# Seven smaller products for a second factor of a Strassen-Winograd projection, with weights split through PSUM

## The chip, the cores and the metric

The kernel runs on one core of a Trainium2 chip. The metric is the device time of one execution in microseconds (us). A core has a matmul engine (TensorE, PE in the profile, with its weight loads as PEld), three engines for elementwise work (VectorE = DVE, ScalarE = ACT, GpSimd = POOL) and SyncE (SP), which issues the DMAs here. Every engine works through its own queue in order; semaphores hold an instruction until what it needs is done. Matmul results go to PSUM, which has eight banks of 128 x 512 float32; everything else lies in SBUF.

## The reference

One layer of a gated short-convolution mixer with a norm before and after. D = 1024, L = 1024 positions, the inner width CI is 2048; all in float32.

```python
def short_conv_mixer(u, w_in, conv_w, w_out):
    z, bg, cg, v = jnp.split(u @ w_in.astype(u.dtype), 4, axis=-1)
    y = bg * causal_dwconv(cg * v, conv_w) * jax.nn.silu(z)
    return y @ w_out.astype(u.dtype)

def reference(x, pre_norm, post_norm, sc_w_in, sc_conv_w, sc_w_out, ...):
    u = rms_norm(x, pre_norm[0])
    m = short_conv_mixer(u, sc_w_in[0], sc_conv_w[0], sc_w_out[0])
    return x + rms_norm(m, post_norm[0])
```

The convolution is depthwise and causal with three taps. Nearly all of the arithmetic is the two projections, 1024 x 1024 by 1024 x 8192 and 1024 x 2048 by 2048 x 1024.

## The kernel before

**Precision.** A float32 product is made of three matmuls in a rounded format (float32r): each operand is split into a high part and a low part, and lo x hi, hi x lo and hi x hi are added in one PSUM bank. `split` does it: ScalarE copies the source into the rounded high part, VectorE subtracts that from the source and leaves the low part (L157 to L159; for the weights of a pair L164 to L175, where the subtraction is L170).

**Tiling of the input projection.** CI is cut into NC = 16 chunks of 128 channels. A chunk needs four column blocks of w_in: for cg and v (the even pair p = 2c) and for z and bg (the odd pair p = 2c + 1). A pair is one 2 x 2 block product, done in Strassen-Winograd form with seven products a, b, c, e, d, f, g instead of eight (`product`, L189). Each has four K blocks times three matmuls, so twelve matmuls of 128 x 128 weights by 512 columns. The activations' combinations UH, UL (names u_a to u_g) are made once; the weights' combinations are made for each pair: `add_s` forms the sums e, c, f and the difference d on POOL (se, sc, sf and raw in the profile; L150, L152, L154, L146). `after` (L215) copies the banks out on ScalarE (`snap`) and adds later products on VectorE: L227 for d, L234 for f, L224 for b. Product f adds into bank pv, which e has begun; the result goes to sn[p, "c"].

**The second level.** From chunk DEEP = 3 on, product b of a chunk's two pairs is taken together: the two pairs' weights for b form a 2 x 2 block matrix, and seven products a' to g' of half size replace the two products. Each is six matmuls of 256 columns (`deep_product`, L728). Their weights' sums are made on POOL (`deep_sums`, ds in the profile, L706 to L710), split in `deep_prep` (dw0, dw1, dw2 of 512 columns and dw3 of 256), and the results are added on VectorE in `deep_after` (L754), which then starts the convolution of the chunk. The factor's own sums are made once under chunk 2 and chunk 3 (`deep_parts`, `deep_subs`, `deep_split`, started from the table UNDER).

**The gate.** When a chunk's even pair is ready, `start_conv` multiplies into gpad (L250 and, for the second half of the positions, L239 on POOL), ScalarE does the first tap (L634) and VectorE the two others (L640). The odd pair gives SiLU(z) (L236, L933) and bg, multiplied in on POOL (L231, L237) and VectorE (L243, L244). The result goes to DRAM (`y_done`). `add_y` then forms its sums for the output projection, one subtraction for chunks below 8 and three from 8 on, of the chunk before.

**w_out.** While the input projection runs, w_out's sums for the second Strassen-Winograd product are also formed: `fetch_t` loads blocks, `add_t` subtracts on VectorE and stores to DRAM (four subtractions per unit; units 0 to 7 are 512 columns wide, L321, units 8 to 15 are 256 wide, L308 to L316). The table TODO says at which pair each unit's turn is.

**Order.** The order of all instructions is written out by hand. The list `slots` is TensorE's order of products. The main loop goes through it: it issues a product, then `prepare(n)` issues the splits of all slots that start within LEAD = 7 (in units in which a full product is 2.72 and a small one 0.72) behind the end of this one, and then the work that follows the product. So each engine's queue follows the slots.

**Memory.** A ring of 36 pages of 128 x 512 float32 (`page`) holds weights, sums and results; a new page waits until the last reader of the one in its place is done. PSUM's eight banks go round in the same way (`bank`).

**Output projection.** Behind chunk 15 comes a second Strassen-Winograd product with y and w_out (L1023 to L1025, with two of its products again by seven smaller ones, L1115 to L1117), and the norm after it.

Of the kernel before, what the change touches and what calls it, by code (L numbers as in the profile page):

```python
# [16 lines left out]
DEEP = 3  # L17
LEAD = 7.0


@with_exitstack
def kernel(
# [144 lines left out]

    def split_low(p, i):
        hi, lo = wt[p, i]
        nc.vector.tensor_sub(lo, source(p, i), hi.bitcast(F32))  # L170

    def split_w(p, kinds):
        for i in kinds if p < len(PAIRS) else "":
            split_high(p, i)
            split_low(p, i)  # L175
# [490 lines left out]

    HH, KQ = HB // 2, KH // 2
    deep, deep_w = {}, {}

    def deep_parts(ks):  # L670

        for k in ks:
            deep[k] = page(f"deep{k}")
            nc.gpsimd.tensor_add(deep[k], UH["b"][:, k].bitcast(F32), UL["b"][:, k].bitcast(F32))

    def deep_subs(ks):

        for k in ks:
            (b11, b12), (b21, b22) = ((t[:, :HH], t[:, HH:]) for t in (deep[k], deep[k + KQ]))
# [7 lines left out]
    def deep_split(i):  # L687
# [3 lines left out]
        if i != "e'":  # L691
            deep[i] = [tmp.tile([P, KQ, HH], F32R, tag="ub", name=f"u{i[0]}{h}_deep", bufs=6) for h in "hl"]
        for k in range(KQ):
            if i == "e'":
                hi, lo = UH["b"][:, k, ls], UL["b"][:, k, ls]
            else:
                hi, lo = (t[:, k] for t in deep[i])
            split(deep[k0 + k][:, ls], hi, lo)

    def deep_sums(c, part):  # L700

        (a11, a12), (a21, a22) = ((t[:, :HH], t[:, HH:]) for t in (block(p, 0, 1) for p in (2 * c, 2 * c + 1)))
        t = page(f"ds{part}_{c}")
        deep[c, part] = t
        if part == 0:
            nc.gpsimd.tensor_add(t[:, :HH], a21, a22)  # L706
            nc.gpsimd.tensor_sub(t[:, HH:], t[:, :HH], a11)
        else:
            nc.gpsimd.tensor_sub(t[:, :HH], a11, a21)
            nc.gpsimd.tensor_sub(t[:, HH:], a12, deep[c, 0][:, HH:])  # L710
# [4 lines left out]
    def deep_prep(c, i):  # L715
        n = DEEP_W[i][0]
        if (c, n) in deep_w:
            return
        if n == 3:
            w = page(f"dw{n}_{c}", F32R, (2, HH))  # L720
            hi, lo, src = w[:, 0], w[:, 1], block(2 * c + 1, 0, 1)[:, HH:]
        else:
            hi, lo = (page(f"dw{n}{h}_{c}", F32R) for h in "hl")
            src = deep.pop((c, n - 1)) if n else block(2 * c, 0, 1)
        split(src, hi, lo)
        deep_w[c, n] = hi, lo

# [506 lines left out]
```

## Time and profile before

| | |
|---|---|
| time, median of 3 runs | 783.65 us (783.64 to 783.88) |
| the profiled execution | 783.5 us, of which span 781.7 us |
| granted TensorE clock, mean | 0.997 |
| ScalarE, POOL busy in the span | 343.2 us, 385.8 us |
| HBM read, written | 91.78 MB, 34.60 MB |

The span goes from the first to the last instruction of the program that the profiler recorded; 1.8 us lie around it. A row of the order in time has the start in us from the span's begin, the duration in us, the engine, the line, the operation, output <- inputs by the program's names (buffer numbers left out), and the shapes; in brackets the idle time before it and what ended that. A duration includes the time for which an instruction that has been started is held up inside the engine. A row of one source line has durations in ns as min/median/max.

### The profile page before, as it was taken

Reading aid. Unit: us, or ns where it says so; the run is one execution under the profiler, and the core shown is the slowest. Engines: PE = TensorE matmul, PEld = TensorE weight load, DVE = VectorE, ACT = ScalarE, POOL = GpSimd, SP = SyncE. Lnnn points to the kernel's source line nnn. Section 1 sums busy time; section 2 is a strip of 40 time slices with the busy share of each in tenths; the row PEclk is TensorE's granted clock in tenths of the full one; section 3 lists DMA queues with packets and bytes.
Section 4 is the critical chain, followed back from the end, with each engine's and each line's share of the span. In section 5 each row is a group of like instructions: output and inputs, shape, how many; then the busy total and the mean of one; then the engine's idle time right before and its main releaser. Section 6 shows DMA issues by size and latency. Waiting matters only on the chain.

```text
span 781.7 us, 11253 instructions
## 1 busy us (share of the span) xinstructions
PE 772.6 (99%) x3852; PEld 656.5 (84%) x3852; DVE 647.1 (83%) x868; ACT 343.2 (44%) x624; POOL 385.8 (49%) x281
## 2 busy tenths in 40 slices
PE   8999999999999999999999999999999999999996
PEld 7888888888888888888888888888888889889985
DVE  6899757969696989898888888896868899986975
ACT  7664434443334343434342434333333575754821
POOL 2506579647474747565565747383838200710041
PEclk9999999999999999999999999999999999999998
DMA  9210431317070738373746455552324979686355
GB/s 323 55 55 14 135 94 55 113 36 231 26 233 23 256 109 256 117 259 126 219 119 205 142 182 166 173 167 95 112 91 138 354 264 386 222 282 206 116 163 188
DMA packets 115817, 127.12 MB, mean 163 GB/s; under 512 B 7416, under 2 KB 74032, under 8 KB 115760
## 3 DMA queue, kind: packets, MB, share of 16 engines
q1 hardware_dynamic: 115744, 126.41, 50.2%
q8 instruction: 30, 0.49, 0.3%
q14 instruction: 27, 0.22, 0.1%
q10 hardware_dynamic: 16, 0.00, 0.0%
HBM read 91.78 MB, written 34.60 MB: 162 GB/s over the span
## 4 chain that ended last, share of the span: by engine, by line
PE 98%; DMA 1%; DVE 0%; ACT 0%; POOL 0%; SPq 0%; issue 0%; DVEq 0%; POOLq 0%; ACTq 0%
PE px L200 14%; PE px L201 14%; PE px L202 14%; PE pv L200 7%; PE pv L202 7%; PE pv L201 7%; PE po_x L1023 4%; PE po_x L1025 4%; PE po_x L1024 4%; PE px L745 2%; PE px L743 2%; PE px L744 2%; PE pp L422 1%; PE po_v L1025 1%; PE po_v L1023 1%; PE po_v L1024 1%
## 5 line engine op out<-in xcount | busy, mean ns | idle before, releaser
L231 POOL TENSOR_TENSOR sne<-sne,cv 128x512 f32<-128x512 f32 x15 | 25.1, 1674 | 149.9 <-DVE sne L227 134.7
L239 POOL TENSOR_TENSOR gpad<-snc,sne 128x512 f32<-128x512 f32 x15 | 25.2, 1678 | 65.8 <-DVE snc L234 65.8
L640 DVE SCALAR_TENSOR_TENSOR cv<-gpad,cw,cv 128x1024 f32<-128x1024 f32 x32 | 42.4, 1325 | 14.7 <-ACT cv L634 14.1
L170 DVE TENSOR_TENSOR wal<-raw,wah 128x512 fp32r<-128x512 f32 x31 | 29.6, 954 | 27.8 <-ACT wah L166 27.8
L152 POOL TENSOR_TENSOR sc<-se,raw 128x512 f32<-128x512 f32 x31 | 50.3, 1621 | 2.4
L154 POOL TENSOR_TENSOR sf<-raw,sc 128x512 f32<-128x512 f32 x31 | 51.4, 1657 | 0.0
L150 POOL TENSOR_TENSOR se<-raw,raw 128x512 f32<-128x512 f32 x31 | 47.3, 1525 | 3.2 <-DMA raw<-in_sc_w_in 3.2
L200 PE MATMUL px<-u_d,wdl 128*128 128x512 f32 x124 | 48.6, 392 | 0.0
L201 PE MATMUL px<-u_d,wdh 128*128 128x512 f32 x124 | 48.4, 391 | 0.0
L200 PE MATMUL px<-u_a,wal 128*128 128x512 f32 x124 | 48.4, 391 | 0.0
L200 PE MATMUL px<-u_g,wgl 128*128 128x512 f32 x124 | 48.4, 390 | 0.0
L201 PE MATMUL px<-u_g,wgh 128*128 128x512 f32 x124 | 48.4, 390 | 0.0
L201 PE MATMUL px<-u_a,wah 128*128 128x512 f32 x124 | 48.4, 390 | 0.0
L202 PE MATMUL px<-u_d,wdh 128*128 128x512 f32 x124 | 48.4, 390 | 0.0
L208 ACT COPY sna<-px 128x512 f32<-128x512 f32 x30 | 17.5, 585 | 70.2 <-PE px L202 47.5
L200 PE MATMUL pv<-u_f,wfl 128*128 128x512 f32 x124 | 48.3, 390 | 0.0
L202 PE MATMUL pv<-u_f,wfh 128*128 128x512 f32 x124 | 48.3, 389 | 0.0
L202 PE MATMUL px<-u_a,wah 128*128 128x512 f32 x124 | 48.2, 389 | 0.0
L201 PE MATMUL pv<-u_f,wfh 128*128 128x512 f32 x124 | 48.2, 389 | 0.0
L200 PE MATMUL px<-u_c,wcl 128*128 128x512 f32 x124 | 48.2, 389 | 0.0
L201 PE MATMUL px<-u_c,wch 128*128 128x512 f32 x124 | 48.2, 389 | 0.0
L202 PE MATMUL px<-u_c,wch 128*128 128x512 f32 x124 | 48.2, 389 | 0.0
(446 smaller groups left out, 2592.7 us busy)
## 6 DMA issues: line engine op xcount, KB each, us to landing
raw<-in_sc_w_in SPq DMA_DIRECT2D x128, 256.0 KB, 4.6
y_d<-cv SPq DMA_DIRECT2D x16, 512.0 KB, 3.1
s_d<-s SPq DMA_DIRECT2D x32, 256.0 KB, 3.1
t<-in_sc_w_out SPq DMA_DIRECT2D x32, 256.0 KB, 4.4
t_d<-t SPq DMA_DIRECT2D x32, 256.0 KB, 3.2
tb<-in_sc_w_out SPq DMA_DIRECT2D x16, 256.0 KB, 4.4
s<-y_d SPq DMA_DIRECT2D x16, 256.0 KB, 4.6
xr<-in_x SPq DMA_DIRECT2D x16, 256.0 KB, 4.4
```

Source lines behind the costliest of these rows:

```text
L150: nc.gpsimd.tensor_add(t, block(p, 1, 0), block(p, 1, 1))
L152: nc.gpsimd.tensor_sub(t, sums[p, "e"], block(p, 0, 0))
L154: nc.gpsimd.tensor_sub(t, block(p, 0, 1), sums[p, "c"])
L170: nc.vector.tensor_sub(lo, source(p, i), hi.bitcast(F32))
L200: nc.tensor.matmul(ps, lo, UH[i][:, k], start=first and k == 0, stop=False, skip_group_check=True)
L201: nc.tensor.matmul(ps, hi, UL[i][:, k], start=False, stop=False, skip_group_check=True)
L202: nc.tensor.matmul(ps, hi, UH[i][:, k], start=False, stop=last, skip_group_check=True)
L239: nc.gpsimd.tensor_mul(gpad[:, TAPS - 1 + HB :], t, sn[p, "e"])
L640: nc.vector.scalar_tensor_tensor(cvs[c], gpad[:, j : j + L], tap(c, j), cvs[c], op0=ALU.mult, op1=ALU.add)
L1023: nc.tensor.matmul(ps, lo, u[:, 0, k], start=first, stop=False, skip_group_check=True)
L1024: nc.tensor.matmul(ps, hi, u[:, 1, k], start=False, stop=False, skip_group_check=True)
L1025: nc.tensor.matmul(ps, hi, u[:, 0, k], start=False, stop=last, skip_group_check=True)
```

## The change

Product f of chunks 4 to 14 (eleven chunks) is done like product b: the two pairs' weights sf form a 2 x 2 block matrix, and seven small products replace two full ones. `deep_parts`, `deep_subs`, `deep_split`, `deep_sums`, `deep_prep` and `deep_product` get the product's letter z as an argument. The small products b' and g' of f add into the banks pv that product e of the pairs has begun; the others have banks of their own. The results are added in a new `deep_after_f`. f's weight sums run on VectorE, b's stay on POOL.

```diff
+DEEP_F = 4
+BY_BANK_DEEP = (("b", 0), ("b", 1), ("f", 0))
...
+    def by_seven(z, c):
+        return c >= DEEP if z == "b" else DEEP_F <= c < NC - 1
...
+    def split_by_bank(src, hi, lo):
+        if not beside_bank:
+            beside_bank.append(bank("beside"))
+        b = beside_bank[0][:, : src.shape[-1]]
+        nc.scalar.copy(hi, src)
+        nc.scalar.copy(b, src)
+        nc.vector.tensor_sub(lo, b, hi.bitcast(F32))
...
     def split_w(p, kinds):
         for i in kinds if p < len(PAIRS) else "":
+            if i in ("ag" if p % 2 else "adg") and by_seven("f", p // 2):
+                wt[p, i] = [page(f"w{i}{h}_{p}", F32R) for h in "hl"]
+                split_by_bank(source(p, i), *wt[p, i])
+                continue
...
+    def deep_sums(z, c, part):
+        eng = nc.gpsimd if z == "b" else nc.vector
...
+        (split_by_bank if (z, n) in BY_BANK_DEEP and by_seven("f", c) else split)(src, hi, lo)
+        deep_w[z, c, n] = hi, lo
...
+        if z == "f" and i in ("b'", "g'"):
+            ps, first = banks[2 * c + (i == "g'"), "v"], False
...
+    def deep_after_f(c, i):
+        p = 2 * c
+        t0, t1 = sn[p, "c"], sn.get((p + 1, "c"))
+        g = gpad[:, TAPS - 1 + HB :]
+        if i in ("b'", "g'"):
+            t, v_ = (t0, banks[p, "v"]) if i == "b'" else (t1, banks[p + 1, "v"])
+            nc.vector.tensor_add(t, v_, t)
+            if i == "b'":
+                nc.gpsimd.tensor_mul(g[:, :HH], t[:, :HH], sn[p, "e"][:, :HH])
+            else:
+                nc.scalar.activation(t, t, AF.Silu)
+                nc.gpsimd.tensor_mul(cvs[c][:, HB:], t, sn[p + 1, "e"])
+            return
+        ps = banks[c, "f" + DEEP_C[i][0]][:, :HH]
+        if i == "d'":
+            both = t1.rearrange("p (a b) -> p a b", a=2)
+            nc.vector.tensor_add(both, ps.unsqueeze(1).broadcast_to([P, 2, HH]), both)
+            return
+        t = (t1 if i == "e'" else t0)[:, slice(0, HH) if i == "a'" else slice(HH, HB)]
+        nc.vector.tensor_add(t, ps, t)
+        if i == "f'":
+            nc.vector.tensor_mul(g[:, HH:], t, sn[p, "e"][:, HH:])
...
-    TODO = {p: j for j, p in enumerate([8, 10, 12, *range(13, 26)])}
+    TODO = {2 * DEEP_F + 2 * j + n: j + n * CH for j in range(CH) for n in (0, 1)}
...
-        sub = {"e": ("a'", "b'"), "a": ("c'", "e'")} if p % 2 == 0 else {"e": ("f'", "d'"), "f": ("g'",)}
-        for i in "cedf":
+        if p % 2 == 0:
+            sub = {"e": "ba bb", "a": "bc be", "d": "fa fb"}
+        elif f7:
+            sub = {"c": "fc fe", "e": "bf ff bd fd", "d": "bg fg"}
+        else:
+            sub = {"e": "bf bd", "f": "bg"}
...
+        for i in "ced" if f7 else "cedf":
...
+        ("d", 2 * DEEP_F - 2): lambda: deep_parts("f", [0]),
...
+        ("g", 2 * DEEP_F): lambda: deep_split("f", "g'"),
...
+            if i == "e'" and by_seven("f", c):
+                deep_sums("f", c, 1)
...
+        if i == "a" and p % 2 and f7:
+            deep_sums("f", p // 2, 0)
...
-            add_s(q, "ec")
+            add_s(q, "ecdf" if f7 else "ec")
...
-    nc = bacc.Bacc("TRN2", target_bir_lowering=False, num_devices=1)
+    nc = bacc.Bacc("TRN2", target_bir_lowering=False, num_devices=1, dynamic_dma_scratch_size=1024)
```

`split_by_bank` makes the low part of eight splits per chunk (a, d and g of the even pair, a and g of the odd pair, dw0 and dw1 of b, dw0 of f) from a copy of the source that ScalarE writes into one PSUM bank, "beside", which all of them share in turn. w_out's units now run at chunks 4 to 11, two in each (unit j at the even pair, j + 8 at the odd one), and their subtractions are issued in twos behind products c and e of an even pair, d of an even pair and a of the odd one. The order of slots in a chunk of the eleven is: c, e, b's a' and b', d, f's a' and b', a of the odd pair, b's c' and e', g; then c, f's c' and e', e, f' and d' of b and f in turn, d, g' of both, a of the next pair, g. The factor of f is summed on POOL under chunk 3 (four additions and eight subtractions) and split in chunk 4. The tile pool for the factors' parts grows from six to fourteen tiles, and the scratch for DMA descriptors is made smaller.

More of the change, by code (lines that the diff above doesn't have):

```diff
@@ L870 @@
     END = len(PAIRS) - 1
-    TODO = {p: j for j, p in enumerate([8, 10, 12, *range(13, 26)])}
-    def odd_t(p, steps):
-        if p % 2 and p in TODO:
-            add_t(TODO[p], steps)
+    TODO = {2 * DEEP_F + 2 * j + n: j + n * CH for j in range(CH) for n in (0, 1)}
     slots = [("a", 2), ("b", 2)]
```

177 lines of the change are left out of this document (98 added, 79 removed).

## The prediction

> **What bounds the kernel now.** I read the page first (busy times, chain), then the sums of single chunks, then the instructions in order of time on one chunk.
>
> ```profile
> span 781.7 us, 11253 instructions
> PE 772.6 (99%) x3852; PEld 656.5 (84%) x3852; DVE 647.1 (83%) x868; ACT 343.2 (44%) x624; POOL 385.8 (49%) x281
> PE 98%; DMA 1%; DVE 0%; ACT 0%; POOL 0%; SPq 0%; issue 0%; DVEq 0%; POOLq 0%; ACTq 0%
> ```
>
> TensorE is never idle and holds 98% of the chain that ended last, so time falls only if it gets less to do, and rises as soon as it has to wait. VectorE (DVE) at 83% is the second engine. In the stage that the change touches it is closer than that. The next rows are one chunk each, from a product g of an odd pair to the next one (columns: length; then busy us and count of PE, PEld, DVE, ACT, POOL; clock; DMA). The first is a shorter stage in which the factor sums of product b are formed.
>
> ```profile
> 130.00:150.00 20.00, 20.00 (x94) 16.50 (x93) 17.58 (x22) 10.34 (x22) 15.30 (x12) 1.00 0.26 77
> ...
> 324.17:361.89 37.72, 37.72 (x187) 32.01 (x186) 34.21 (x42) 14.10 (x26) 22.74 (x16) 1.00 0.58 188
> 399.63:437.36 37.73, 37.73 (x187) 32.02 (x186) 32.72 (x44) 14.12 (x26) 22.47 (x16) 1.00 0.54 168
> ```
>
> A chunk takes 37.73 us and TensorE fills it; VectorE is busy 33 to 34 of it. How far VectorE runs ahead is seen at the low part that is closest to its use:
>
> ```profile
> 434.06 0.68 DVE L170 TENSOR_TENSOR wgl<-raw,wgh 128x512 fp32r<-128x512 f32 x1
> 437.36 0.39 PE L200 MATMUL px<-u_g,wgl 128*128 128x512 f32 x1
> ```
>
> It ends at 434.74, 2.6 us before TensorE reads it. That lead is all that can be lost before TensorE stands still.
>
> **Part 1: TensorE's work.** Eleven chunks lose the two full products f (24 matmuls of 512 columns) and get 42 of 256 columns.
>
> ```profile
> 405.07 0.39 PE L200 MATMUL pv<-u_e,wel 128*128 128x512 f32 x1
> 407.79 0.28 PE L743 MATMUL px<-u_b,dw0l 128*128 128x256 f32 x1
> 409.22 0.40 PE L200 MATMUL px<-u_d,wdl 128*128 128x512 f32 x1
> 411.97 0.39 PE L200 MATMUL pv<-u_f,wfl 128*128 128x512 f32 x1
> ...
> 647.79 0.28 PE L1115 MATMUL pb_x<-oB_b,oA_b 128*128 128x256 f32 x1
> 656.06 0.28 PE L1115 MATMUL pb_x<-oB_b,oA_b 128*128 128x256 f32 x1
> ```
>
> Starts, not durations, give the cost, since matmuls overlap. The twelve full ones take 407.79 - 405.07 = 2.72 us, the twelve small ones 1.43 (0.119 each), and the twelve full ones behind them 2.75, that is 0.03 more. The last two rows lie 69 small matmuls apart: 0.120 each in a long run too, so longer runs of small ones cost no more. Per chunk: 2 x 2.72 = 5.44 goes, 42 x 0.119 = 5.00 comes, and two more changes from small to full add 0.06. The gain is 0.38 us, 4.1 us over eleven chunks, and a chunk then wants 37.73 - 0.38 = 37.35 us. By itself this gives 783.5 - 4.1 = 779.4.
>
> **Part 2: VectorE's own work.** What one instruction takes of the engine when nothing holds it is seen where they follow each other:
>
> ```profile
> 417.13 0.69 DVE L170 TENSOR_TENSOR wcl<-sc,wch 128x512 fp32r<-128x512 f32 x1
> 417.73 0.68 DVE L234 TENSOR_TENSOR snc<-pv,snc 128x512 f32<-128x512 f32 x1
> 418.33 0.68 DVE L170 TENSOR_TENSOR wel<-se,weh 128x512 fp32r<-128x512 f32 x1
> 418.93 0.42 DVE L754 TENSOR_TENSOR sna<-px,sna 128x256 f32<-128x256 f32 x1
> 419.26 0.41 DVE L754 TENSOR_TENSOR sna<-pv,sna 128x256 f32<-128x256 f32 x1
> ```
>
> 0.60 us for 512 columns, 0.335 for 256 (half the columns cost more than half the time), from PSUM or SBUF alike. The two taps of the convolution take 2.53 together (rows below, 431.53 to 434.06).
>
> Before, chunk 10 has 25 instructions of 512, 16 of 256 and the taps: 15.0 + 5.4 + 2.5 = 22.9 us, though it shows 32.72 busy. The 9.8 between is time held by POOL (part 3).
>
> Counted in the changed program, chunks 5 to 8 each have 29 of 512, 22 of 256 and the taps: 17.4 + 7.4 + 2.5 = 27.3. In 9 to 11 two more subtractions (`add_y` has three there instead of one) make 28.5. Chunk 4, which also splits the factors of f (eight of 256), has 28 and 30: 29.4. Chunks 12 to 14, without w_out's sums, have 27 and 18: 24.7. Against chunk 10 of before that is +5.6: the four sums `deep_sums` of f now on VectorE, seven adds with a multiply in place of two adds, and 3.5 splits of f in place of two.
>
> **Part 3: what POOL holds.** VectorE and POOL shut each other out when both read two SBUF tensors:
>
> ```profile
> 400.76 1.74 POOL L237 TENSOR_TENSOR cv<-snc,sne 128x512 f32<-128x512 f32 x1
> 402.46 1.74 POOL L154 TENSOR_TENSOR sf<-raw,sc 128x512 f32<-128x512 f32 x1
> 404.15 1.19 POOL L706 TENSOR_TENSOR ds<-raw 128x256 f32<-128x256 f32 x1
> ...
> 401.54 1.51 DVE L159 TENSOR_TENSOR dw0l<-raw,dw0h 128x512 fp32r<-128x512 f32 x1 [0.19 <-ACT dw0h L158]
> 402.97 1.77 DVE L170 TENSOR_TENSOR wdl<-raw,wdh 128x512 fp32r<-128x512 f32 x1
> 404.67 0.68 DVE L243 TENSOR_TENSOR cv<-px,cv 128x512 f32<-128x512 f32 x1
> ...
> L170 DVE TENSOR_TENSOR wdl<-raw,wdh x31: 674/1773/1777, 47.4 to 611.9; 128x512 fp32r<-128x512 f32 x31
> L227 DVE TENSOR_TENSOR sne<-px,sne x30: 676/682/692, 73.6 to 621.6; 128x512 f32<-128x512 f32 x30
> L150 POOL TENSOR_TENSOR se<-raw,raw x31: 1283/1728/1747, 26.2 to 597.5; 128x512 f32<-128x512 f32 x31
> ```
>
> They alternate: dw0l, issued at 401.54, gets its turn as L237 ends at 402.50; sf waits for it, and wdl then waits until sf ends at 404.20. A subtraction of two SBUF tensors takes 674 ns free and 1777 behind a POOL instruction, so a full meeting costs 1.1 us; one that arrives halfway I take as 0.55, one behind a 256-column POOL instruction as 1.19 - 0.60 = 0.6. One source in PSUM (L227) never takes over 692. So the eight splits that now read the bank copy are free of it; that is real help.
>
> The Trainium skill (SBUF — State Buffer, "SBUF: two separate sides") says the pair of ports is locked for the whole of an instruction. By it a full meeting would cost POOL's undisturbed 1.28 rather than the 1.1 measured, some 1.3 us more per chunk and some 10 more on the sum; the measured price is used.
>
> I walked the changed order of chunk 9 along VectorE and POOL. POOL first runs ten instructions nearly without pause (two products, four sums of b, then se, sc, raw, sf of the odd pair). wel, L265's product and three of w_out's subtractions meet it: 0.55 + 0.55 + 0.55 + 1.1 + 0.55 = 3.3. The second burst is gpad's half and se, sc, raw, sf of the next pair, released one by one as VectorE frees the buffers they write. Around it stand the sums of f, wel and dwf2l: 0.6 + 0.75 + 0.75 + 1.1 + 1.1 = 4.3. Together 7.6. Bounds: 4 (half of these meetings) and 9.8 (as before). I take 7.6, the walk.
>
> **Part 4: round trips to ScalarE.** VectorE issues in order, so it stands where its next instruction needs a ScalarE result that itself needs VectorE's last one.
>
> ```profile
> 429.63 0.68 DVE L250 TENSOR_TENSOR gpad<-px,sna 128x512 f32<-128x512 f32 x1
> 430.34 1.16 ACT L634 ACTIVATE cv<-gpad,cw 128x1024 f32<-128x1024 f32 x1 [2.02 <-DVE gpad L250]
> 431.53 2.61 DVE L640 SCALAR_TENSOR_TENSOR cv<-gpad,cw,cv 128x1024 f32<-128x1024 f32 x2 [0.89 <-ACT cv L634]
> 434.06 0.68 DVE L170 TENSOR_TENSOR wgl<-raw,wgh 128x512 fp32r<-128x512 f32 x1
> 435.86 0.68 DVE L234 TENSOR_TENSOR snc<-pv,snc 128x512 f32<-128x512 f32 x1
> 436.57 0.63 ACT L236 ACTIVATE snc<-snc 128x512 f32<-128x512 f32 x1 [4.05 <-DVE snc L234]
> 437.63 0.60 ACT L166 CAST weh<-se 128x512 fp32r<-128x512 f32 x1
> 438.27 0.81 DVE L170 TENSOR_TENSOR wel<-se,weh 128x512 fp32r<-128x512 f32 x1 [0.90 <-ACT weh L166]
> ```
>
> Before, other work stood between. Now: the convolution comes straight after gpad, 431.53 - 429.63 - 0.60 = 1.3 idle. SiLU, weh and wel follow the last add of f directly, 0.71 + 0.54 + 0.64 - 0.60 = 1.3. All bank copies share one bank, so ScalarE's next copy waits for VectorE's last subtraction: dwb0l then wdl 0.7, dwb1l then wgl 0.3, and 0.4 at dwb0l, behind three ScalarE steps. dwf1's high part waits for the sum just made: 0.7. Sum 4.7. Behind each of these waits stand the low parts for TensorE. A ScalarE copy into PSUM is not in the trace; I take weh's 0.60, the nearest row. Were it 0.4, three of the round trips would shrink by 0.2, some 4 us on the sum; were it 0.8, as much the other way. An add that reads a PSUM half twice (product d' of f) is not in it either and is put at L234's 0.60; at 0.335 it would take 2 us off the sum, and nothing speaks for more than 0.60. ScalarE itself has room: 14.1 us of 37.7, plus some 6.
>
> **Part 5: edits costed at nothing.** POOL's twelve sums of f's factors in chunk 3 lie under TensorE as b's did (130 to 150: PE 20.00 of 20); without that cover they would cost part of the lead. raw of pair p+2 is now issued on SP behind stores that wait for w_out's subtractions, some 10 us into the chunk; it is read some 19 us in. The smaller DMA scratch only makes room for tiles.
>
> **The sum.** VectorE's demand is own work + 7.6 + 4.7: 41.7 in chunk 4, 39.6 in 5 to 8, 40.8 in 9 to 11, 37.0 in 12 to 14. Over the 37.35 that TensorE wants: 4.35 + 4 x 2.25 + 3 x 3.45 = 23.7 us. Of this 3 is absorbed by the lead (2.6 at the closest place; 3, since the order there changes). So TensorE stands 20.7 us: 783.5 - 4.1 + 20.7 = 800. The profiled execution's 783.5 lies 0.15 below the median, which changes nothing.
>
> **Rivals.** (a) TensorE stays the bound, as the change intends: the bank copies clear so many meetings that POOL holds VectorE for less than 5.5 us a chunk. With H us held, the excess of the eight chunks is 8 x H - 37.1, and it exceeds lead and gain together (7.1) from H = 5.5 on: that is the point that decides. At 5 chunk 4 has 1.75 and chunks 9 to 11 have 0.85 each, 4.3 less the lead 1.3: 780.7; at 4 it is 779.4. For it: eight splits, the dearest among them (1.77 for wdl), become 0.68. Against it: VectorE still has 29 instructions of two SBUF tensors per chunk (30 before), and POOL 15 as before, one of them now half as long.
> (b) Between: 6 us held, 8 x 6 - 37.1 = 10.9, less the lead 7.9: 787.
> (c) POOL holds as long as before, 9.8: 41.3, less the lead 38.3: 818. For it: both engines have as many such instructions as before; against it: theirs are shorter.
> (d) The banks decide: with one of eight given to the copies, product a of the next chunk writes a bank that VectorE reads after f'. By the walk 1.6 us remain there, so it waits only where VectorE is late anyway, and adds nothing to 800.
>
> **How the numbers follow.** Forecast 800 (its own range 790 to 811, which is 6.3 to 9.0 us held): 0.50. (a) 0.27. (b) with what lies around it, 783 to 790: 0.14, of which 0.04 is within 0.2% (1.6 us, what can be told from no change). (c) 0.09. Faster 0.27, same 0.04, slower 0.69. The range 779 to 812 leaves out most of (c) and a little below (a).
>
> **What would show it.** Right: chunks 5 to 11 take 39 to 41 us instead of 37.7, TensorE has gaps in them ended by VectorE at wel, dwb2l and dwf2l of the odd pair, VectorE is busy or waiting on ScalarE throughout, and chunks 12 to 14 are near 37.4. Wrong: the chain is still 98% TensorE and chunks take 37.35 (then part 3 or 4 is too dear); or chunks of small products take more than 37.35 without gaps (part 1); or the gaps are ended by ScalarE, POOL or DMA.

## The result, and the profile after

| | before | after |
|---|---|---|
| time, median (6 runs each) | 783.91 us (783.64 to 785.47) | 827.89 us (826.64 to 828.75) |
| the profiled execution, span in it | 783.5 us, 781.7 us | 826.6 us, 824.8 us |

The changed kernel takes 1.0557 times as long (95% interval 1.0543 to 1.0571). The direction was forecast, the size was not: 44 us were lost instead of 16.5, above the range. The page of the changed kernel, in the lines that answer to those of before:

```profile
span 824.8 us, 11904 instructions
PE 783.6 (95%) x4050; PEld 665.1 (81%) x4050; DVE 696.9 (84%) x1008; ACT 400.5 (49%) x742; POOL 354.1 (43%) x293
PE 37%; DVE 20%; issue 8%; ACT 5%; DMA 3%; POOL 1%; DVEq 0%; POOLq 0%; SPq 0%; ACTq 0%
```

TensorE went from 98% of the chain that ended last to 37%, and VectorE stands in it with 20%. Busy shares alone would not have said so: VectorE's is 84% of the span, against 83% before. The stretches say where. The first fence has one chunk of before, the second has chunks 4, 6, 10 and 13 of the changed kernel, each from product g of an odd pair to the next (columns as before: length; busy us and count of PE, PEld, DVE, ACT, POOL; clock; DMA share; GB/s):

```profile
324.16:361.89 37.73, 37.73 (x187) 32.02 (x186) 34.22 (x42) 14.11 (x26) 22.75 (x16) 1.00 0.58 188
```

```profile
172.95:217.56 44.61, 40.44 (x205) 34.23 (x203) 38.17 (x61) 21.76 (x43) 25.29 (x21) 0.92 0.43 139
299.66:340.70 41.04, 38.44 (x205) 32.29 (x205) 36.53 (x54) 19.05 (x35) 18.58 (x15) 1.00 0.47 151
425.98:471.41 45.43, 39.57 (x205) 33.50 (x205) 37.94 (x56) 19.14 (x35) 18.66 (x15) 0.96 0.49 159
515.99:554.58 38.59, 37.85 (x205) 32.45 (x205) 32.43 (x48) 19.04 (x35) 18.01 (x15) 1.00 0.34 103
```

Every one of the eleven chunks is longer than 37.73. Chunk 4 takes 44.6 us, 5 to 8 take 41.0 to 41.1, 9 to 11 take 44.2, 45.4 and 44.6, 12 to 14 take 38.4 to 38.6. Their excess over 37.73 is 6.9 + 13.3 + 21.0 + 2.4 = 43.6 us, and the spans differ by 43.1: the whole loss lies in these chunks.

What TensorE waits for in the changed kernel (us in total, times, longest):

```profile
PE px L221 <- ACT sna L229: 20.6, 8, 4.9
PE px L221 <- DVE sne L248: 5.9, 11, 1.0
PE pv2f L776 <- DVE snc L807: 4.5, 7, 0.9
```

None of these three is a weight that comes late (the first that is, dwb2l, follows with 1.1 us). A product that adds into a bank must wait until the partial sum in it has been copied out or added: L229 is ScalarE's snapshot behind product a, L248 VectorE's addition behind d, L807 those of f's small products. That gave two readings of the trace. **Theory V**: VectorE's demand is too long, as forecast, and the waits show up wherever an instruction happens to stand in its queue. **Theory S**: the order in which these readings are issued costs the time; moved forward, it is gone. A third, **theory B**: the one bank for the copies chains ScalarE and VectorE together and costs more than it spares.

### The profile page after: what moved, and what is told of

Read it like the earlier page. It is cut to its first block, busy times and chain, and to the rows that moved or that the text cites. A ratio compares the mean times of both kernels' runs of the same rounds, so it can differ in the third digit from the quotient of the medians.

```text
span 824.8 us, 11904 instructions
## 1 busy us (share of the span) xinstructions
PE 783.6 (95%) x4050; PEld 665.1 (81%) x4050; DVE 696.9 (84%) x1008; ACT 400.5 (49%) x742; POOL 354.1 (43%) x293
## 3 DMA queue, kind: packets, MB, share of 16 engines
q1 hardware_dynamic: 115744, 126.41, 47.3%
## 4 chain that ended last, share of the span: by engine, by line
PE 37%; DVE 20%; issue 8%; ACT 5%; DMA 3%; POOL 1%; DVEq 0%; POOLq 0%; SPq 0%; ACTq 0%
PE px L221 4%; PE po_x L1105 4%; PE po_x L1107 4%; PE po_x L1106 4%; PE px L222 3%; PE px L223 3%; DMA s<-y_d 3%; ACT beside L182 1%; DVE t L342 1%; DVE sne L248 1%; DVE dsf L734 1%; DVE sna L783 1%; DVE snc L807 1%; PE pv L222 1%; PE pv L221 1%
## 5 line engine op out<-in xcount | busy, mean ns | idle before, releaser
L252 POOL TENSOR_TENSOR sne<-sne,cv 128x512 f32<-128x512 f32 x15 | 20.9, 1396 | 153.1 <-DVE sne L248 137.9
L221 PE MATMUL px<-u_c,wcl 128*128 128x512 f32 x124 | 52.1, 420 | 20.6 <-ACT sna L229 20.6
L152 POOL TENSOR_TENSOR se<-raw,raw 128x512 f32<-128x512 f32 x31 | 44.1, 1422 | 31.1 <-DVE t L334 12.8
L187 DVE TENSOR_TENSOR wel<-se,weh 128x512 fp32r<-128x512 f32 x31 | 37.6, 1213 | 19.1 <-ACT weh L168 19.1
L182 ACT COPY beside<-raw 128x512 f32<-128x512 f32 x66 | 38.9, 590 | 30.0 <-DVE dwf0l L183 14.5
L222 PE MATMUL px<-u_c,wch 128*128 128x512 f32 x124 | 51.0, 411 | 0.0
L223 PE MATMUL px<-u_c,wch 128*128 128x512 f32 x124 | 51.0, 411 | 0.0
L222 PE MATMUL px<-u_g,wgh 128*128 128x512 f32 x124 | 48.5, 392 | 0.0
L222 PE MATMUL px<-u_a,wah 128*128 128x512 f32 x124 | 48.5, 391 | 0.0
L222 PE MATMUL pv<-u_e,weh 128*128 128x512 f32 x124 | 48.4, 390 | 0.0
L221 PE MATMUL pv<-u_e,wel 128*128 128x512 f32 x124 | 48.4, 390 | 0.0
L223 PE MATMUL px<-u_g,wgh 128*128 128x512 f32 x124 | 48.3, 389 | 0.0
L223 PE MATMUL pv<-u_e,weh 128*128 128x512 f32 x124 | 48.3, 389 | 0.0
L221 PEld LDWEIGHTS px<-u_c,wcl 128*128 128x128 f32 x124 | 24.8, 200 | 29.1 <-ACT sna L229 24.0
```

The costliest lines, as they stand in the source:

```text
L152: nc.gpsimd.tensor_add(t, block(p, 1, 0), block(p, 1, 1))
L182: nc.scalar.copy(b, src)
L221: nc.tensor.matmul(ps, lo, UH[i][:, k], start=first and k == 0, stop=False, skip_group_check=True)
L222: nc.tensor.matmul(ps, hi, UL[i][:, k], start=False, stop=False, skip_group_check=True)
L223: nc.tensor.matmul(ps, hi, UH[i][:, k], start=False, stop=last, skip_group_check=True)
```

## The experiments

All runs took one execution each, on chips where the kernel before took 782.96 to 783.96 us. Lengths of chunks in us, worked out from the starts of product g of the odd pairs:

| run | time | chunk 4 | 5 to 8 | 9 to 11 | 12 to 14 |
|---|---|---|---|---|---|
| changed kernel, profiled | 826.64 | 44.6 | 41.0 to 41.1 | 44.2, 45.4, 44.6 | 38.4 to 38.6 |
| e1_snap_first | 826.54 | 46.4 | 39.6 to 41.0 | 45.5, 44.4, 44.4 | 38.5 to 38.6 |
| e2_s_first | 823.18 | 44.6 | 41.0 to 41.3 | 42.9, 44.4, 43.1 | 38.5 to 38.7 |
| e3_no_bank | 844.2 | 47.9 | 42.5 to 42.6 | 46.2, 47.9, 45.5 | 39.2 to 39.5 |
| e4_no_wout | 807.54 | 41.6 | 38.6 | 42.1, 43.0, 42.3 | 38.4 to 38.6 |
| e5_no_wout_reads | 795.04 | 41.0 | 38.6 to 38.7 | 38.6 | 38.1 to 38.6 |
| e6_taps_late | 836.85 | 45.5 | 42.0 to 42.4 | 45.1, 45.7, 45.0 | 39.4 to 39.6 |
| e7_no_pool_sums | 798.07 | 38.7 | 38.6 | 40.7, 40.5, 40.2 | 38.1 to 38.6 |
| e8_f_from_12 | 794.53 | 37.7 | 37.7 | 37.7, 38.2, 41.0 | 44.5, 38.5, 38.1 |
| e9_order | 808.75 | 45.3 | 39.2, 39.6, 39.8, 41.2 | 41.2, 41.4, 40.2 | 37.3, 37.8, 37.8 |
| e10_order_no_wout | 786.39 | 40.5 | 37.3, 37.8, 37.9, 37.9 | 37.8 | 37.8 |
| e11_f_sums_pool | 836.77 | 45.5 | 41.6 to 42.7 | 45.3, 47.3, 45.4 | 39.3, 38.6, 38.6 |
| e12_e_by_bank | 820.48 | 43.1 | 39.9 to 40.2 | 43.9, 44.1, 44.5 | 38.8 to 39.0 |
| e13_bare | 793.74 | 46.2 | 37.8 | 37.8 to 37.9 | 37.8 to 37.9 |
| e14_spread | 814.53 | 45.8 | 38.1, 39.4, 37.3, 37.8 | 37.8, 39.6, 37.3 | 39.6, 39.1, 39.1 |

**Is it the order of the readings?** e1 moves ScalarE's snapshot of product a of the odd pair ahead of the splits:

```diff
         product(p, i)
+        early = i == "a" and p % 2 and f7
+        if early:
+            after(p, i)
         prepare(n)
-        after(p, i)
+        if not early:
+            after(p, i)
```

> Moves one ScalarE copy: the snapshot of product a of the odd pair is issued ahead of the splits that are prepared behind that product, so it no longer stands behind dwf1's high part. Theory V (VectorE's demand of own work, POOL's holds and round trips sets the length of chunks 4 to 11): the wait of 20.6 us at product c goes, but VectorE's sequence is as long as before, the gaps move to other products, and the time falls by 3 us at most (824 to 828). Rival S (what sets it are the reads of a bank that the next product adds to, and above all this one): the wait is on the path and the time falls by 15 to 20 us (808 to 812).

826.54 us: nothing gained. TensorE's 20.6 us of waiting for the snapshot are gone, and in their place stand waits for VectorE:

```profile
PE pv2b L776 <- DVE dwb2l L161: 9.5, 7, 1.7
PE pv2f L776 <- DVE snc L807: 9.0, 9, 1.8
PE pv L221 <- DVE wel L187: 4.0, 4, 1.7
```

As the main cause of these 44 us, theory S falls. The mean clock is lower in e1 (0.979 against 0.989); but in chunks 6 to 8, where both runs show 1.00, it takes 39.6, 40.9 and 40.8 us against 41.0 each, 1.8 us less in three chunks, where theory S asked for some 2 in each. The wait moves within the chunk, as it must where VectorE sets the pace. That VectorE does so can be read in the trace of the changed kernel: from 172.95 to 515.99 us, chunks 4 to 11, its waits are ended by ScalarE (37.1 us) and by loads (4.9 us), and none by TensorE.

**The y that comes late.** In chunks 9 to 11 `add_y` waits for y's earlier chunk, which SP issues behind w_out's stores. e2 puts `fetch_s` first in the work behind product c of the even pair:

```diff
+            if p % 2 == 0 and p > 2:
+                fetch_s(prev)
             if p % 2 == 0 and p in TODO:
                 add_t(TODO[p], [0, 1])
                 fetch_t(TODO[q])
-            if p % 2 == 0 and p > 2:
-                fetch_s(prev)
```

> Issues the two loads of y's earlier chunk on SP ahead of w_out's stores and loads. Theory V: the idle time of VectorE at add_y's first addition (2.2 us in chunk 10) goes from chunks 9 to 11, which become about 42 to 43 us; the time falls by 4 to 6.5 us (821 to 824). Rival S: nothing but chunks 9 to 11 can change, and they wait for the snapshot anyway: under 1 us.

823.18 us, within V's range: chunks 9 to 11 fall by 0.99 to 1.47 us, the others stay within 0.2. Chunk 10, at 44.4, stays above the 42 to 43 expected: another load on the same queue takes over part of the wait there. First VectorE's row of the changed kernel (in brackets the idle time before it and what ended it), then that of e2:

```profile
445.75 0.69 DVE L299 TENSOR_TENSOR s<-s,cv 128x512 f32<-128x512 f32 x1 [2.22 <-DMA s<-y_d]
```

```profile
443.53 0.43 DVE L332 TENSOR_TENSOR t<-tb,tb 128x256 f32<-128x256 f32 x1 [1.60 <-DMA tb<-in_sc_w_out]
```

**Are the bank copies worth it?** e3 makes all low parts from SBUF again:

```diff
     def split_by_bank(src, hi, lo):
...
         nc.scalar.copy(hi, src)
-        nc.scalar.copy(b, src)
-        nc.vector.tensor_sub(lo, b, hi.bitcast(F32))
+        nc.vector.tensor_sub(lo, src, hi.bitcast(F32))
```

> Makes the eight low parts per chunk from SBUF again; the PSUM copies are left out, everything else stays. Theory V: the round trips at wdl and wgl go (1.0 us a chunk), but up to five of the eight meet POOL at 1.1 us each, so a chunk gets 2 to 5 us longer and the time rises to 840 to 870. Rival B (the one shared bank and its extra copies cost more than they bring): a chunk gets 1 to 2 us shorter, 805 to 817.

844.2 us, and every chunk of the eleven is longer. The copies spare 844.2 - 826.6 = 17.6 us. Theory B falls.

**VectorE's own work.** e4 leaves out w_out's subtractions:

```diff
         for n, a, b in [((1, 1, 0), (3, 3, 1), (0, 3, 0), (2, 2, 3))[n] for n in steps]:
-            nc.vector.tensor_sub(t[n], t[a], t[b])
             nc.sync.dma_start(t_d[:, n, j], t[n])
```

and likewise for the units of 256 columns.

> Leaves out the subtractions of w_out's sums on VectorE (loads and stores stay, the stored blocks are the plain ones, so the output is another). Theory V: 3.7 us of own work and two to three meetings go from chunks 4 to 11; chunks 5 to 8 become like 12 to 14, 38.6, chunks 9 to 11 some 40: the time is 798 to 806. Rival S: the order of banks and snapshots is the same, so the gaps stay and the time falls by under 8 us (over 819).

807.54 us, 1.5 above the expected 798 to 806: without the subtractions VectorE reaches `add_y` earlier and waits longer there, 12.0 us in three chunks. The clean reading is in chunks 5 to 8. They lose 2.45 us, less than the 3.7 of work taken away, and stop at 38.6, where the unchanged chunks 12 to 14 stand too. So a second limit lies at 38.6, above the 37.35 that was forecast for TensorE. e5 (e4, e2's order, and five readings ahead of the splits) was to find it:

> As e4 (w_out's subtractions left out), with two changes of order besides: y's earlier chunk is loaded ahead of w_out's stores, and five readings of a bank that a later product adds into (snapshot of product a of the odd pair, the addition behind d of the even pair, those behind f's a', c', e') are issued ahead of the splits. Theory R (the 38.6 us that chunks 5 to 8 and 12 to 14 of e4 still take are TensorE waiting for such readings, not its own work): chunks 5 to 14 take 37.4 to 37.9 us, chunk 4 about 41, in all 784 to 789 us. Theory P (TensorE itself needs 38.6 us for such a chunk, since its small products cost more than the 0.12 us forecast): chunks 5 to 8 and 12 to 14 stay at 38.5 or more, 794 to 800 us.

795.04 us and chunks of 38.6: theory R missed, and theory P's numbers came (but for 38.1 in chunk 14). Its reason did not: TensorE still waits, once in each of the eleven chunks and for one thing above all, the addition L248 behind d of the odd pair. In the waits of e5 it comes first:

```profile
PE px L221 <- DVE sne L248: 9.9, 11, 1.0
```

The five readings weren't the ones that count. What does count is in VectorE's order in chunk 13 of the changed kernel, ahead of TensorE's product g:

```profile
547.56 0.68 DVE L271 TENSOR_TENSOR gpad<-px,sna 128x512 f32<-128x512 f32 x1
549.52 2.61 DVE L661 SCALAR_TENSOR_TENSOR cv<-gpad,cw,cv 128x1024 f32<-128x1024 f32 x2 [1.27 <-ACT cv L655]
552.04 0.68 DVE L183 TENSOR_TENSOR wgl<-beside,wgh 128x512 fp32r<-128x512 f32 x1
552.64 0.68 DVE L804 TENSOR_TENSOR snc<-px2f,snc 128x512 f32<-128x512 f32 x1
553.24 0.68 DVE L187 TENSOR_TENSOR wcl<-sc,wch 128x512 fp32r<-128x512 f32 x1
553.84 0.68 DVE L248 TENSOR_TENSOR sne<-px,sne 128x512 f32<-128x512 f32 x1
```

```profile
554.58 0.50 PE L221 MATMUL px<-u_g,wgl 128*128 128x512 f32 x1 [0.34 <-DVE sne L248]
```

g adds into the bank that L248 (the addition behind d of the odd pair) still has to read. L248 stands behind the whole convolution: gpad, the round trip to ScalarE's tap, two taps and three more instructions, and that chain begins at a product of TensorE itself. It is too long however much room VectorE has elsewhere. e9, below, moves L248 and tests this.

**The round trips.** e6 tried to fill the 1.27 us at the tap, by issuing VectorE's two taps behind the addition of f's d':

```diff
-        for j in range(1, TAPS - (c == NC - 1)):
+        for j in range(1, 1 if late else TAPS - (c == NC - 1)):
             conv_tap(c, j)
...
             nc.vector.tensor_add(both, ps.unsqueeze(1).broadcast_to([P, 2, HH]), both)
+            for j in range(1, TAPS):
+                conv_tap(c, j)
             return
```

> VectorE's two taps of the convolution are issued behind the addition of f's d' instead of directly behind the product into gpad, so that other work stands in the round trip to ScalarE's first tap. Theory V (a chunk is as long as VectorE's own work, POOL's holds and the round trips together): the 1.27 us that VectorE waits there in each of chunks 4 to 11 go, less at most 0.3 that other waits take back; chunks 5 to 8 take 39.8 to 40.2 instead of 41.04, in all 816 to 819 us. Rival (VectorE's waits are slack and the length comes from elsewhere, banks or readings): 825 us or more, since the gate's multiplications come later.

836.85 us, 10 us slower: V missed, and the rival's 825 or more came, but not for its reason. The trace tells why:

```profile
337.27 0.68 DVE L271 TENSOR_TENSOR gpad<-px,sna 128x512 f32<-128x512 f32 x1
340.22 0.69 DVE L183 TENSOR_TENSOR wgl<-beside,wgh 128x512 fp32r<-128x512 f32 x1 [2.27 <-ACT beside L182]
340.83 0.68 DVE L805 TENSOR_TENSOR snc<-px2f,snc 128x512 f32<-128x512 f32 x1
```

wgl came to the front of VectorE's queue, and its bank copy stands on ScalarE behind that same tap: 2.27 us of waiting instead of 1.27. The chunk grew by 1.0, to 42.06. One us more of waiting on VectorE is one us more of chunk, as V has it; but L248 stands behind the same wait, so this run doesn't tell V from the chain above.

e9 does it right. f's d' is added ahead of the splits, ScalarE makes weh before the two SiLUs, the readings of d, a and f's a', c', e' go ahead of the splits, y's load is first:

```diff
+            early = z == "f" and i in ("a'", "c'", "e'", "d'")
+            if early:
+                deep_after_f(c, i)
             prepare(n)
             if z == "f":
-                deep_after_f(c, i)
+                if i == "g'" and (2 * c + 2, "e") not in wt:
+                    split_high(2 * c + 2, "e")
+                    ahead.add((2 * c + 2, "e"))
+                if not early:
+                    deep_after_f(c, i)
...
+        early = f7 and i in ("ad" if p % 2 else "d")
+        if early:
+            after(p, i)
         prepare(n)
```

> All work as in the changed kernel, in another order: y's earlier chunk loaded first (as in e2); the addition of f's d' stands in the round trip to ScalarE's first tap, ahead of the splits (in e6 it stood behind the low part of g, whose bank copy waits behind that tap); ScalarE's weh ahead of the two SiLUs; and the readings of banks that a later product adds into (snapshot of a of the odd pair, d of both pairs, f's a', c', e') ahead of the splits. Theory V: VectorE loses 0.6 and 1.2 us of waiting per chunk, so chunks 5 to 8 take 39.0 to 39.8, 9 to 11 take 41 to 42.8; theory R2 (the 38.6 of a chunk in which VectorE has room is the chain from b's d' over gpad, the tap, the two taps, wgl, f's d', wcl to the addition of d of the odd pair, for which g waits): chunks 12 to 14 take 37.4 to 37.8. In all 803 to 811 us. Rival (order moves nothing, as in e1): 820 or more and 38.6 in chunks 12 to 14.

808.75 us, within the expectation, with all of the work done. Chunks 5 to 7 take 39.2 to 39.8 (8, at 41.2, missed its 39.8; see the last section), and chunk 12 shows the floor gone: TensorE busy without a break for 37.31 us.

```profile
297.21:336.98 39.77, 37.81 (x205) 32.43 (x204) 35.31 (x54) 19.15 (x35) 19.27 (x16) 1.00 0.49 156
500.93:538.24 37.31, 37.31 (x206) 32.34 (x204) 28.83 (x47) 19.15 (x35) 17.69 (x15) 1.00 0.35 107
```

The gain in the first row is not the one that was meant. VectorE's waits for ScalarE add up to 4.1 us in this chunk, and to 4.2 in the changed kernel's chunk 6. What fell is its busy time, 35.31 against 36.53: in the new order it meets POOL less (the first wel takes 0.69 us instead of 1.45). e9 makes all its moves at once; apart from y's load (e2), what each of them gives was not tested.

e10 is e9 without w_out's subtractions:

> e9 with w_out's subtractions left out, which takes 3.7 us of work from VectorE in each of chunks 4 to 11. Theories V and R2: VectorE's demand falls below what TensorE wants, chunks 5 to 14 take 37.35 to 37.8, chunk 4 about 40 to 41, in all 780 to 786 us: the TensorE gain of 0.38 us a chunk is then seen bare. If TensorE's small products cost more than 0.12 us, or a wait of another kind is left, the chunks stay at 38 or more (788 or more in all).

786.39 us, hardly above the expectation. Chunk 5 takes 37.31, the others 37.8: they lose 0.5 us at the first product c. It waits for the snapshot of a of the even pair (in chunk 9 ScalarE ends it at 367.65 us, and c starts at 367.70), which stands behind the two SiLUs.

**POOL's holds.** e7 leaves out POOL's sums se, sc, raw and sf of chunks 4 to 14, with VectorE's instructions as they are (`t = block(p, 0, 0)` for each of the four kinds).

> POOL's four sums of each pair of chunks 4 to 14 (se, sc, raw, sf) are left out; the splits take raw blocks in their place. VectorE's own instructions are the same as in the changed kernel. Theory V: with eight of POOL's 512-column instructions per chunk gone, most of the 8.7 us that POOL holds VectorE in a chunk go (about 3 left); chunks 5 to 8 fall to the floor of 38.4 to 38.8 seen in e4, 9 to 11 to 38.6 to 41, in all 795 to 804 us. Rival (VectorE's own work and its round trips alone are too long, POOL's holds are small): 818 us or more.

798.07 us. The row of chunk 8, to be held against chunk 6 of the changed kernel above, has the same 54 instructions on VectorE:

```profile
327.75:366.34 38.59, 37.60 (x204) 32.40 (x204) 29.63 (x54) 19.16 (x35) 6.73 (x7) 1.00 0.51 160
```

They are busy for 29.6 us instead of 36.5. So 6.9 us per chunk were time in which POOL's sums held VectorE's instructions, and in chunks 4 to 8 all excess above the floor goes with them.

e11 runs f's four weight sums on POOL instead (`eng = nc.gpsimd` for both products).

> The four sums of f's weights per chunk (256 columns each) run on POOL instead of VectorE, all else as in the changed kernel. Theory V: VectorE loses 1.34 us of own work and some 1.6 of holds (L733 and L734 take 2.9 together where 0.84 would do free), against which stand new meetings of up to 0.6 for each of the four; chunks 5 to 8 take 38.8 to 40.5, in all 805 to 822 us. Rival (POOL, at 18.6 of 41 us busy, is late with the sums, since its bursts are in order): 826 or more, with TensorE waiting for dwf1 and dwf2.

836.77 us: V's number missed, the rival's came. POOL issues in order and was still waiting to multiply into gpad; only then does it make the sums, and VectorE waits for them (32.9 us at dwf1l in all). TensorE's longest waits are not at dwf1 and dwf2, as the rival had it, but at the snapshot of a (29.0 us), which stands behind dwf1's high part on ScalarE. POOL's row, then VectorE's:

```profile
322.73 0.73 POOL L796 TENSOR_TENSOR gpad<-snc,sne 128x256 f32<-128x256 f32 x1 [7.04 <-DVE snc L794]
```

```profile
325.64 1.22 DVE L161 TENSOR_TENSOR dwf1l<-dsf,dwf1h 128x512 fp32r<-128x512 f32 x1 [2.99 <-ACT dwf1h L160]
```

e12 makes e's low part from the bank too (`"aeg"` and `"adeg"` in `split_w`).

> The low part of product e of both pairs is made from the bank copy too (wel reads PSUM). Theory V: wel takes 0.68 instead of 1.45 in both pairs, 1.5 us per chunk; one more ScalarE step of 0.5 in each round trip that shares the one bank takes back up to 1.3. Chunks 5 to 8 take 39.5 to 40.8, in all 812 to 824 us. Rival (the one shared bank already sets the pace, as each copy waits for VectorE's last subtraction): 826 or more.

820.48 us, as V expected; chunks 5 to 8 lose 1 us each.

**Fewer chunks, and other places for w_out.** e8 does f by seven in chunks 12 to 14 alone (`DEEP_F = 12`, w_out's units as in the changed kernel, e5's order).

> Product f by seven only in chunks 12 to 14 (its factors summed under chunk 11 and split in chunk 12), the readings and y's load in the order of e5, w_out's units two per chunk in 4 to 11. Theory V: chunks 4 to 11 have the product f of before and take 37.7 to 38, 13 and 14 take 37.4, chunk 12 with eight more splits 38 to 40; in all 782.5 to 786 us. If the new schedule of w_out is itself what costs, chunks 4 to 11 take over 38.5 and the time is over 790.

794.53 us, 8.5 above the expectation, from chunks 11 and 12. Chunks 4 to 9, with w_out's new schedule but the old f, take exactly 37.73: that schedule alone costs nothing. What costs are the two chunks in which f's factors are summed and split, +3.2 us in chunk 11 and +6.7 in chunk 12. Chunks 13 and 14, at 38.5 and 38.1, gain nothing either: e5's order leaves the chain to L248 as it is.

```profile
361.58:399.31 37.73, 37.73 (x187) 32.02 (x186) 34.92 (x43) 13.53 (x25) 21.62 (x15) 1.00 0.60 192
478.50:522.95 44.45, 40.08 (x205) 33.93 (x205) 37.53 (x58) 21.99 (x44) 25.69 (x22) 0.96 0.29 89
```

e13 (e10 with the even pair's snapshot of a moved too, and f's factors made half a chunk earlier) and e14 (all of w_out's work, eight of its units in chunks 1 to 3, one a chunk in eight later ones) were to beat the kernel before:

```diff
-        ("d", 2 * DEEP_F - 2): lambda: deep_parts("f", [0]),
+        ("e", 2 * DEEP_F - 2): lambda: deep_parts("f", [0]),
...
-        ("c", 2 * DEEP_F): lambda: deep_split("f", "c'"),
+        ("d", 2 * DEEP_F - 1): lambda: deep_split("f", "c'"),
...
-    TODO = {2 * DEEP_F + 2 * j + n: j + n * CH for j in range(CH) for n in (0, 1)}
+    whole = [s for s in slots if not s[2:]]
+    for j, n in ((0, 2), (1, 6), (8, 10), (2, 14), (3, 18), (4, 22), (9, 26), (5, 30)):
+        turn_t(j, whole[n], whole[n + 3], whole[n + 5])
```

(`turn_t` loads unit j at the first slot and subtracts in twos at the others; the last four lines are e14's.)

> e10 (w_out's subtractions left out) with two more moves: the snapshot of product a of the even pair is issued ahead of the splits too, and the sums and splits of f's factors come some half a chunk earlier (the splits late in chunk 3 instead of in chunk 4). Theory R2 (what e10 still loses per chunk, 0.48 before product c, is the wait for that snapshot): chunks 5 to 14 take 37.3 to 37.45; the splits out of chunk 4 take it from 40.5 to 37.5 to 39, chunk 3 may take up to 1 more. In all 779 to 783 us, which shows the TensorE gain of 0.38 to 0.42 a chunk bare. Rival (small products next to full ones cost TensorE more than forecast): chunks stay at 37.7 or more, 785 or more in all.

> e13 with all of w_out's subtractions in again, but ten of the 16 units moved: eight units in chunks 1 to 3 (before f is done by seven), the other eight one to a chunk in 5 to 8, 10 and 12 to 14. Nothing is left out. Theory V: VectorE has some 8 us of room in chunk 1 and 12 in chunk 2, so those units cost nothing there; in the others a unit of 1.3 to 2.4 us of VectorE's work fits under the room that e13 leaves. In all 780 to 786 us, chunks with a unit 37.4 to 38.5. If w_out's loads and stores or the meetings with POOL in the early chunks cost: chunks 1 and 2 longer than 43.5 and 35.4, 788 or more.

Both missed, at 793.74 and 814.53 us. In e13 the snapshot of a moved ahead of the splits but not of the two SiLUs, so chunks 5 to 14 stay at 37.8: the rival's number, though chunk 12 of e9 shows that TensorE needs 37.31. In chunk 4 TensorE waits 6.2 us for it at the first product c, as those SiLUs wait 5.7 and 2.9 us for VectorE. In e14 chunks 2 and 3 grow from 35.4 and 38.0 to 40.4 and 48.2 us; VectorE is busy 14.2 and 14.4 us longer than before the change, with 13 and 11 instructions more, and POOL, which makes the factors there, 2.8 and 15.2 us. So the early chunks had no such room, as the second reading named in advance (788 or more) had it. No run beats the kernel before: even e10, with w_out's 30 us of VectorE work left out, stays 3.4 us above it.

## Why the prediction was right in direction and wrong in size

The mechanism was right: VectorE, with its holds and round trips, sets the pace of chunks 4 to 11. The step that failed is the sum along VectorE, and the lead taken off it. Part 3's holds were mis-sized, 8.6 us a chunk instead of 7.6. Three things were put at nothing: loads that come late (5.3 us in chunks 9 to 11), the later start of an instruction that reads its neighbour's result (0.5 to 0.7 a chunk), and readings of banks that TensorE waits for (38.5 us instead of 37.35 in chunks 12 to 14). And of the 3 us of lead only 1.2 were there.

**Part 1 (TensorE's work) holds.** Forecast: 37.35 us a chunk, 0.38 less than before. Chunk 12 of e9 takes 37.31 with TensorE busy throughout. Small and full matmuls side by side cost what their starts had said.

**Part 2 (VectorE's own work) holds but for one thing.** The instructions cost 0.60 and 0.335 us as forecast. The sum left out that an instruction which reads the result of the one before it starts later:

```profile
442.65 0.42 DVE L329 TENSOR_TENSOR tb<-tb 128x256 f32<-128x256 f32 x1
443.10 0.43 DVE L332 TENSOR_TENSOR t<-tb,tb 128x256 f32<-128x256 f32 x1
...
446.47 0.69 DVE L300 TENSOR_TENSOR s<-s,s 128x512 f32<-128x512 f32 x1
447.20 0.69 DVE L301 TENSOR_TENSOR s<-cv,s 128x512 f32<-128x512 f32 x1
```

443.10 - 442.65 = 0.45 instead of 0.335, and 447.20 - 446.47 = 0.73 instead of 0.60. In chunk 6 that is 0.5 us (four such pairs, and the taps), in 9 to 11, with two more pairs, 0.7.

**Part 3 (POOL's holds) was too small.** Forecast 7.6 us a chunk; in chunk 6, from start to start, they come to 41.0 less 27.3 of own work, 4.6 of round trips and 0.5 for those neighbours, 8.6. The second burst was sized well (4.4 against 4.3; L733, L734 and dwb2l below are three of its meetings). The first was not, 4.2 against 3.3: wel and L265, taken as met halfway at 0.55 each, waited 0.95 and 1.16.

```profile
301.74 1.45 DVE L187 TENSOR_TENSOR wel<-se,weh 128x512 fp32r<-128x512 f32 x1 [1.21 <-ACT weh L168]
303.29 0.69 DVE L183 TENSOR_TENSOR dwb0l<-beside,dwb0h 128x512 fp32r<-128x512 f32 x1
...
305.96 1.83 DVE L265 TENSOR_TENSOR cv<-cv,sna 128x512 f32<-128x512 f32 x1
307.72 0.68 DVE L183 TENSOR_TENSOR dwf0l<-beside,dwf0h 128x512 fp32r<-128x512 f32 x1
...
324.59 1.44 DVE L733 TENSOR_TENSOR dsf<-sf,sf 128x256 f32<-128x256 f32 x1
325.96 1.51 DVE L734 TENSOR_TENSOR dsf<-sf,dsf 128x256 f32<-128x256 f32 x1
327.39 1.78 DVE L161 TENSOR_TENSOR dwb2l<-dsb,dwb2h 128x512 fp32r<-128x512 f32 x1
```

The starts give it: 303.29 - 301.74 - 0.60 = 0.95, and 307.72 - 305.96 - 0.60 = 1.16.

**Part 4 (round trips) holds** in chunks 5 to 8: 4.7 forecast, and in chunk 6 VectorE is idle for 4.2 (1.27, 1.21, 0.74, 0.66 and 0.32; the 0.4 at dwb0l did not come), which is 4.6 from start to start, as the prediction reckoned. In chunk 4 it is 6.9. The bank copy, taken at weh's 0.60, took 0.59.

**Part 5 failed for SP.** It asked for raw alone whether a load that is issued later still comes in time. y's earlier chunk was moved behind the same stores and does not: 2.22 us idle in chunk 10, 4.0 in chunks 9 to 11 together, and 0.9 more for a block of w_out; 5.3 from start to start.

**Little of the lead was there.** 3 us were to be absorbed, since VectorE had made wgl 2.6 us ahead of its use. But g also waits for L248, which stands behind wgl in VectorE's queue. From L248 to L248 VectorE's chunk 4 takes 216.82 - 171.01 = 45.8 us, TensorE's, from g to g, 44.6: 1.2 were absorbed. After the change TensorE waits for readings of banks, and a reading can't be made ahead: it begins when TensorE's own product ends. In chunks 12 to 14 the same chain makes a chunk 38.5 us long, where 37.35 was forecast, though VectorE has room. Rival (d) looked for such a wait at product a and priced it at nothing; it sits at g (L248), at f' (L807) and at the snapshot of a. As e1 shows, those waits cost next to nothing where VectorE is late anyway, so (d) was right for chunks 5 to 11 and not for 12 to 14.

**The gap of 27 us, by term,** along VectorE from start to start. Chunks 5 to 8 are 1.45 longer than forecast each (5.8): 1.0 from POOL's holds, 0.5 from the neighbours. Chunks 9 to 11 are 3.9 longer each (11.8): 1.7 from these two, 1.8 from the loads, 0.5 from one more wait for ScalarE (last section). Chunk 4 is 4.1 longer (45.8 against 41.7), of which 2.2 are round trips and 1.2 own work. Chunks 12 to 14 are some 1.2 longer each (3.5), by the chain to g. 1.8 of the lead were missing. Together 27.0, and 826.6 - 800 = 26.6.

By the prediction's own sum 8.6 us held give 779.4 + 8 x 8.6 - 37.1 - 3 = 808, so the holds alone are 8 of the 27. Rival (a), TensorE staying the bound, asked for under 5.5 us held; 8.6 were. Rival (c) came nearest in time with 818, but with more held (9.8) than was; and its sum left out that chunks 12 to 14, at 24.7 + 9.8 + 4.7 = 39.2 us, would then pass 37.35 too, 5.5 us in all.

The signs named in advance read badly. Chunks 5 to 8 at 41.0 are at the edge of the 39 to 41 given, 9 to 11 at 44.2 to 45.4 beyond it, and 12 to 14 at 38.5 are not near 37.4. The gaps stand at product c, f' and g instead of at wel, dwb2l and dwf2l, where they appear only once the snapshot is moved (e1). The largest are ended by ScalarE, which the prediction had named as a sign against it. But the snapshot stands behind dwf1's high part on ScalarE, which waits for VectorE's sum (50.8 us in chunks 4 to 11), and e1 showed that moving it gains next to nothing.

## What to carry to other kernels

Where one engine is 99% busy and a second one 83%, price a change by what it adds to the second, with the time that others hold it, stage by stage: here 0.42 us of TensorE a chunk was bought with 5.6 us of VectorE work and its holds, in a chunk where VectorE had some 4 us to give. List each reading of a PSUM bank that a later product adds into: such a reading can't be done ahead, so what stands in its queue is on the critical path even where the engine has room. A wait that vanishes without the time falling (e1) shows an engine that is late everywhere; look for what it is busy with, not for the next wait.

## What the runs showed of the hardware

**TensorE's clock halves after waits.** In chunk 4 of the changed kernel, product c after a wait of 3.18 us ran at half the granted clock: 5.28 us from its first matmul to the next product's instead of 2.72. The row of the stretch (clock: the third number from the end) and its first matmul:

```profile
197.00:202.20 5.20, 5.20 (x12) 4.10 (x13) 5.20 (x12) 2.81 (x7) 1.28 (x1) 0.50 0.34 125
```

```profile
196.98 0.79 PE L221 MATMUL px<-u_c,wcl 128*128 128x512 f32 x1 [3.18 <-ACT sna L229]
```

The Trainium skill (TensorE: Matmul & The Clock Gate, "What's actually happening") says that the clock goes to half after an idle window of about 3.4 us and comes back after as long a busy one. The half agrees. But less idle time is enough: e9 also shows it after two waits of 0.91 and 0.89 us with product work between them. The second row is that stretch, in chunk 8; the first is the same place one chunk earlier, where waits of 1.07 and 0.89 us left the clock alone:

```profile
327.90:331.20 3.30, 3.30 (x23) 3.12 (x24) 3.27 (x9) 0.17 (x1) 0.00 (x0) 1.00 0.73 207
367.60:371.00 3.40, 3.40 (x19) 3.40 (x20) 3.21 (x8) 0.09 (x2) 0.00 (x0) 0.59 0.80 221
```

Chunk 8 took 41.2 us, chunk 7 39.8. What decides is how the waits fall on a fixed grid. The clock records of e9's trace put the starts of its half-clock stretches in chunks 4 to 10 at 207.77, 368.20, 409.16 and 450.12 us, that is 47, 12 and 12 steps of 3.413 us apart, and the eight other runs with more than one such stretch show such a grid too. Cut the twelve runs that have half-clock stretches into these steps, from 60 to 640 us: the 44 steps at full clock that half clock follows have 1.66 to 3.41 us of idle time on TensorE each, and the other 1940 have 1.68 at most. In e9 both waits fall into the step from 364.79 to 368.20, 1.7 us in all. One chunk earlier the grid parts them, 1.3 and 0.6. So in these runs idle time of half a step, in one wait or in several, brings the half clock.

In the changed kernel the slow products cost little: VectorE, which sets the pace, never waits for TensorE in chunks 4 to 11. ScalarE does, at its snapshot of product e in chunks 4 and 9 to 11, and the bank copy for wal behind it is then late for VectorE by 0.6, 0.5, 0.5 and 0.3 us, 1.9 in all.
